# Changing the order of the tokens round a recurrence: in the matmuls' moving side instead of in copies and products

## The chip, the core and the metric

The kernel runs on one NeuronCore of a Trainium2 chip. A core has five engines that run side by side and meet at semaphores: TensorE (PE: matrix products out of SBUF into PSUM; its weight loads are listed as PEld), VectorE (DVE: elementwise work), ScalarE (ACT: functions of one argument), GpSimd (POOL) and SyncE (SP), of which the last two mostly issue DMAs here. SBUF and PSUM hold 128 partitions; an instruction names a pattern of elements along the partition, the same for all 128. The metric is the device time of one execution in microseconds (us).

A matmul has a stationary side, 128 x 128 weights that are loaded into the array, and a moving side, here up to 512 columns, which is read from SBUF and streamed past the weights. The result of each column is added up in a PSUM bank. The products here are in float32 precision: each operand is split into a high part (rounded to the type fp32r) and a low part, and every product is three matmuls: high x high, high x low, low x high.

## What is computed

One decoder layer on 512 tokens of width 1024: a SwiGLU layer, a mixer, another SwiGLU layer, each with norms around it. The mixer runs an attention branch and a recurrent branch on the same normed input `u` and merges them with gates. Only the recurrent branch matters here:

```python
xc  = causal_conv4(u @ w_in[:, xr], conv_w) + conv_b      # width 4, along the tokens
gate_x, gate_a = sigmoid(heads(xc) @ w_x + b_x), sigmoid(heads(xc) @ w_a + b_a)
log_a = -8 * gate_a * softplus(-a_param)
a, b  = exp(log_a), sqrt(-expm1(2 * log_a)) * gate_x * xc
h_t   = a_t * h_{t-1} + b_t                               # the recurrence, token by token
rec   = h * gelu(u @ w_in[:, yr])
rec_d = rec @ w_rec_branch
merged = gate0 * attn_d + gate1 * rec_d                   # gates from u @ w_in[:, gl]
```

The convolution and the recurrence run along the tokens, so they need the tokens in the order of time. The matrix products before and after do not care for the order.

## The kernel before

Activations are kept transposed: features on the 128 partitions, the 512 tokens along the free dimension. The tokens are not in the order of time there. Token number 4 i + p stands in column 128 p + i (p = 0 to 3, i = 0 to 127), an order that suits the dilated attention. Call it phase order; the other one is the order of time. Two views translate between them: `pi` reads a tile of 512 columns as (p, i) with 128 neighbours in the inner dimension, `ip` reads it as the same (p, i) where neighbouring i are four floats (16 bytes) apart.

The stage of the recurrent branch begins at about 638 us and ends at about 836 us of the span. Its order is written out (line 1493 on): `conv(0)`, and then for each of four heads `branch`, the load of the head's gate weights, `conv` of the next head, `gates_of`, `recur`, and some of the merge gates (line 1504). After the last head come the eight products with `w_rec_branch` (line 1512). Each head has two blocks of 128 features, so each of these routines works on two tiles of 128 x 512.

- `gemm` (lines 294 to 298) multiplies a block of 8 x 128 x 128 weights with the eight tiles of an activation: for each of eight tiles three matmuls of 512 columns (lines 279 to 281), 24 matmuls in all, into one PSUM bank.
- `conv` (line 1419): one `gemm` of `um`, the normed input in phase order; ScalarE copies the bank into `xr`, reading phase order and writing the order of time (line 1427, through `ip` and `pi`). The rest of the convolution is one ScalarE and three VectorE operations, then `split` makes high and low parts of the result in `rec` (lines 264, 265).
- `branch` (line 1435): one `gemm` of `um`; VectorE copies the bank into `ge`, which stays in phase order (line 1443).
- `gates_of` (line 1447): the head's small matmuls on `rec`, in the order of time, and sigmoids.
- `recur` (line 1463): elementwise work in the order of time, then the scan (line 1489) into `th`. Line 1490 multiplies `th`, read through `ip`, with `ge`, and writes `ge`: from here on everything is in phase order again. `split` writes it over `rec` (line 1491).
- Line 1504: the merge gates, `gemm` of `um`, sigmoid; phase order throughout.
- Lines 1512 to 1515: `gemm` of `rec`, the multiply with the merge gate in `sig` and the sum with the attention branch, all in phase order.

Weights come in by DMA in one stream, through two `raw` buffers (line 210); `fetch` splits them into high and low parts, with ScalarE and VectorE, some way ahead of their use. A planner places each engine's instructions from its own costs and from the priorities in the code; copies out of PSUM have a raised one (`EVAC`).

Of the kernel before, what the change touches and what calls it, by code (L numbers as in the profile page):

```python
# [12 lines left out]
AF = mybir.ActivationFunctionType  # L13
# [4 lines left out]
T = 512  # L18
# [131 lines left out]
def hybrid_layer(ctx: ExitStack, tc: tile.TileContext, xT: bass.AP, xN: bass.AP, wst: bass.AP,  # L150
                 first: bass.AP, rows: bass.AP, wdn: bass.AP, wbig: bass.AP, consts: bass.AP, bias: bass.AP, out: bass.AP):
    nc = tc.nc
    DVE, ACT, PE = nc.vector, nc.scalar, nc.tensor
# [68 lines left out]
    def fetch(key, slot=None, ahead=0):  # L222

        with tc.high_priority(offset=ahead if slot else AHEAD):
            src = raw_of(key)
            w = src.shape[-1]
            t = slot() if slot else w8() if w > 512 else w4()
            split(t[:, 0, :w], t[:, 1, :w], src)
            return t[:, 0, :w], t[:, 1, :w]

    def w8():
        return wpool.tile([P, 2, 1024], F32R, name="w8", tag="w8", bufs=4)
# [45 lines left out]
    def mm3(ps, wh, wl, xh, xl, first, last):  # L278
        PE.matmul(ps, wh, xh, start=first, stop=False)  # L279
        PE.matmul(ps, wh, xl, start=False, stop=False)  # L280
        PE.matmul(ps, wl, xh, start=False, stop=last)  # L281
# [9 lines left out]
        ts = [big([P, 2, 2, T]) for _ in range(4)]  # L291
        return Act([ts[k // 2][:, 0, k % 2, :] for k in range(8)], [ts[k // 2][:, 1, k % 2, :] for k in range(8)])

    def gemm(ps, wt, x, sl=slice(0, T), n=None):
        n = n or x.n
        a, b = k128(wt[0], n), k128(wt[1], n)
        for k in range(n):
            mm3(ps, a[:, k, :], b[:, k, :], x.hi[k][:, sl], x.lo[k][:, sl], k == 0, k == n - 1)

    def gemm_first(keys, x, slots, then):  # L300

# [443 lines left out]
    class Home:  # L745
# [15 lines left out]
        def slot(self, i):  # L761
            return self.act[:, 2 * i:2 * i + 2, :]
# [368 lines left out]
    um = act_of(um_t[:2], um_t[2:])  # L1131
# [15 lines left out]
    with ExitStack() as mx:  # L1147
# [228 lines left out]
        for c in range(KC):  # L1376
            ps = acc_ps()
# [3 lines left out]
    with ExitStack() as mx:  # L1381
        rpool = mx.enter_context(tc.tile_pool(name="rec", bufs=1))
        rec_t = rpool.tile([P, 16, T], F32R, name="rec")
        rec = Act([rec_t[:, i, :] for i in range(8)], [rec_t[:, 8 + i, :] for i in range(8)])
        sig = rpool.tile([P, KC, T], F32, name="sig")
        lpool_cm = tc.tile_pool(name="lru", bufs=1)
        lpool = lpool_cm.__enter__()


        def s8(name):  # L1390
            return lpool.tile([P, 8], F32, name=name)
        o, w = SMALL["ap"]
        av = sm[:, o:o + w]
        na, ab, ex, zz, z2, po = (s8(n) for n in ("na", "ab", "ex", "zz", "z2", "po"))
        sp4, sp8 = s8("sp4"), s8("sp8")
        DVE.tensor_scalar(na, av, -1.0, None, op0=ALU.mult)
        DVE.tensor_tensor(ab, av, na, op=ALU.min)
        ACT.activation(ex, ab, AF.Exp)
        DVE.tensor_scalar(zz, ex, 2.0, None, op0=ALU.add)
        DVE.reciprocal(zz, zz)  # L1400
        DVE.tensor_mul(zz, zz, ex)
        DVE.tensor_mul(z2, zz, zz)
        DVE.memset(po, 1.0 / 19.0)
        for i in (17, 15, 13, 11, 9, 7, 5, 3, 1):
            DVE.tensor_mul(po, po, z2)
            DVE.tensor_scalar(po, po, 1.0 / i, None, op0=ALU.add)
        DVE.tensor_mul(po, po, zz)
        DVE.tensor_scalar(na, na, 0.0, None, op0=ALU.max)
        DVE.scalar_tensor_tensor(po, po, 2.0, na, op0=ALU.mult, op1=ALU.add)
        DVE.tensor_scalar(sp4, po, 4.0, None, op0=ALU.mult)  # L1410
        DVE.tensor_scalar(sp8, po, -8.0, None, op0=ALU.mult)

        def ip(ap):
            return ap.rearrange("q (i p) -> q p i", p=4)

        def pi(ap):
            return ap.rearrange("q (p i) -> q p i", p=4)

        def conv(hd):

            for c in (2 * hd, 2 * hd + 1):
                ps = acc_ps()
                gemm(ps, fetch(("in", 36 + c)), um)
                xr = lpool.tile([P, 3 + T], F32, name="xr", tag="xr", bufs=2)
                DVE.memset(xr[:, 0:3], 0.0)
                with tc.high_priority(offset=EVAC):
                    ACT.activation(ip(xr[:, 3:]), pi(ps), AF.Copy)
                xc = sig[:, c, :]
                ACT.activation(xc, xr[:, 3:], AF.Identity, bias=col("cb", c), scale=col("cw", 3 * 8 + c))
                for t in (2, 1, 0):  # L1430
                    DVE.scalar_tensor_tensor(xc, xr[:, t:t + T], col("cw", t * 8 + c), xc,
                                             op0=ALU.mult, op1=ALU.add)
                split(rec.hi[c], rec.lo[c], xc)

        def branch(hd):

            gel = []
            for c in (2 * hd, 2 * hd + 1):
                ps = acc_ps()
                gemm(ps, fetch(("in", 44 + c)), um)  # L1440
                ge = lpool.tile([P, T], F32, name="ge", tag="ge", bufs=4)
                with tc.high_priority(offset=EVAC):
                    DVE.tensor_copy(ge, ps)
                gel.append(ge)
            return gel

        def gates_of(hd, wh, wl):
            a_ = wh.rearrange("p (w i c) -> p w i c", w=2, i=2)
            b_ = wl.rearrange("p (w i c) -> p w i c", w=2, i=2)
            gs = {}  # L1450
            for w, bn in ((1, "ba"), (0, "bx")):
                for j in range(2):
                    ps = aux_ps()
                    for i in range(2):
                        js = slice(j * P, (j + 1) * P)
                        mm3(ps, a_[:, w, i, js], b_[:, w, i, js], rec.hi[2 * hd + i], rec.lo[2 * hd + i],
                            i == 0, i == 1)
                    g = lpool.tile([P, T], F32, name="gt", tag="gt", bufs=6)
                    ACT.activation(g, ps, AF.Sigmoid, bias=col(bn, 2 * hd + j))
                    gs[w, j] = g  # L1460
            return [gs[1, j] for j in range(2)], [gs[0, j] for j in range(2)]

        def recur(hd, gel, gas, gxs):

            cs = (2 * hd, 2 * hd + 1)
            ths, rs = [tmp("th") for _ in cs], [tmp("r0") for _ in cs]
            for c, th, ga in zip(cs, ths, gas):
                ACT.activation(th, ga, AF.Tanh, scale=sp4[:, c:c + 1])  # L1470
            for c, r0, ga in zip(cs, rs, gas):
                ACT.activation(r0, ga, AF.Exp, scale=sp8[:, c:c + 1])
            for r0, th, ga in zip(rs, ths, gas):
                ACT.activation(r0, r0, AF.Copy, bias=0.5, scale=0.5)
                DVE.scalar_tensor_tensor(ga, th, 1.0, r0, op0=ALU.add, op1=ALU.mult)
                DVE.scalar_tensor_tensor(r0, ga, 2.0, r0, op0=ALU.subtract, op1=ALU.mult)
                DVE.tensor_mul(ga, th, r0)
            for c, gx in zip(cs, gxs):
                DVE.tensor_mul(gx, gx, sig[:, c, :])
            for th in ths:  # L1480
                ACT.activation(th, th, AF.Sqrt)
            for ga in gas:
                ACT.activation(ga, ga, AF.Copy, bias=1.0, scale=2.0)
            for ge in gel:
                ACT.activation(ge, ge, AF.Gelu_apprx_tanh)
            for c, r0, th, ga, gx, ge in zip(cs, rs, ths, gas, gxs, gel):
                DVE.scalar_tensor_tensor(th, th, -2.0, r0, op0=ALU.mult, op1=ALU.mult)
                DVE.tensor_mul(gx, gx, th)
                DVE.tensor_tensor_scan(th, ga, gx, 0.0, op0=ALU.mult, op1=ALU.add)
                DVE.tensor_mul(pi(ge), ip(th), pi(ge))  # L1490
                split(rec.hi[c], rec.lo[c], ge)

        turns.update(n=4, of=(4, 5, 6, 7), aux=0)
        conv(0)
        for hd in range(NH):
            gel = branch(hd)
            lru = fetch(("lru", hd))
            if hd + 1 < NH:
                conv(hd + 1)
            gas, gxs = gates_of(hd, *lru)  # L1500
            recur(hd, gel, gas, gxs)
            for c in GATE1[hd]:
                ps = acc_ps()
                gemm(ps, fetch(("in", 60 + c)), um)
                ACT.activation(sig[:, c, :], ps, AF.Sigmoid)
        lpool_cm.__exit__(None, None, None)
        turns.update(n=5, of=(5, 6, 7))

        mg = act_big("mg")
        for c in range(KC):  # L1510
            ps = acc_ps()
            gemm(ps, fetch(("rec", c)), rec)
            DVE.tensor_mul(sig[:, c, :], ps, sig[:, c, :])
            DVE.tensor_add(sig[:, c, :], sig[:, c, :], facc[:, c, :])
            split(mg.hi[c], mg.lo[c], sig[:, c, :])
# [149 lines left out]
```

## Time and profile before

| | |
|---|---|
| median of 2 runs | 1230.96 us (1230.32 to 1231.6) |
| the profiled execution | 1229.78 us, of it the span 1228.0 us |
| granted TensorE clock, mean over the span | 0.998 |
| busy: TensorE, weight loads, VectorE, ScalarE | 1213.7, 1094.4, 961.2, 740.6 us |
| stage of the recurrent branch | 637.7 to about 836 us |

The profile is that of one execution, whose span runs from the first to the last instruction. A row of a group of instructions gives the line, the engine and operation, output <- inputs, shape and count, then the busy time in us and the mean duration of one in ns, then the time that the engine stood idle just before such instructions and who ended it. A row of a wait reads: engine, tile and line <- who released it: total us, times, longest us. The timeline lists start and duration in us. Matmuls overlap each other, so that the duration of one (390 ns) is longer than the step from one to the next.

### The profile page before, as it was taken

How to read it: one execution, taken by the hardware profiler on the slowest of the kernel's cores; microseconds unless marked ns; L12 is line 12 of the kernel's file. 1: busy time of each engine (PE TensorE's matmuls, PEld its weight loads, DVE VectorE, ACT ScalarE, POOL GpSimd, SP SyncE). 2: the span in 40 equal slices, each digit the busy share in tenths (PEclk: the TensorE clock that was granted, in tenths of full speed). 3: DMA queues.
4: the chain of work that ended last, by engine and by line, in shares of the span. 5: the costliest groups of instructions: out<-in, count | busy, mean ns of one | idle time of the engine just before them, and what ended most of it. 6: DMA issues, size and time to landing. Idle time of an engine off the chain costs nothing.

```text
span 1228.0 us, 18986 instructions
## 1 busy us (share of the span) xinstructions
PE 1213.7 (99%) x7556; PEld 1094.4 (89%) x7556; DVE 961.2 (78%) x1504; ACT 740.6 (60%) x1229; POOL 75.6 (6%) x123
## 2 busy tenths in 40 slices
PE   9999999999999999999999999999999999999997
PEld 8898989999878999999988878888899999999996
DVE  7998778988579888888566878655788887979864
ACT  6566665655556564666545878734566665656452
POOL 0001111100102000000000000000110010101000
PEclk9999999999999999999999999999999999999999
DMA  6336646464725322222252222324463555455441
GB/s 245 137 104 172 170 110 175 142 164 119 258 103 166 115 91 91 78 78 104 85 190 73 99 103 69 133 77 166 147 197 104 152 155 153 151 146 159 117 155 69
DMA packets 36025, 163.40 MB, mean 133 GB/s; under 512 B 3936, under 2 KB 7136, under 8 KB 23904
## 3 DMA queue, kind: packets, MB, share of 16 engines
q1 hardware_dynamic: 18288, 107.13, 24.9%
q0 software_dynamic: 17648, 55.06, 17.4%
q8 instruction: 59, 0.97, 0.3%
q14 instruction: 30, 0.25, 0.1%
HBM read 151.69 MB, written 6.29 MB: 129 GB/s over the span
## 4 chain that ended last, share of the span: by engine, by line
PE 84%; DVE 8%; ACT 4%; issue 2%; DMA 2%; SPq 0%; DVEq 0%; ACTq 0%
PE bank L972 9%; PE bank L973 9%; PE bank L974 9%; PE bank L281 5%; PE bank L279 5%; PE bank L280 5%; PE bank L639 4%; PE bank L640 4%; PE bank L641 4%; PE bank L887 4%; PE bank L886 4%; PE bank L888 4%; PE bank L393 3%; PE bank L392 3%; PE bank L394 3%
## 5 line engine op out<-in xcount | busy, mean ns | idle before, releaser
L265 DVE TENSOR_TENSOR w<-raw,w 128x1024 fp32r<-128x1024 f32 (+1 forms) x273 | 295.4, 1093 | 68.7 <-ACT w L264 65.0
L264 ACT ACTIVATE w<-raw 128x1024 fp32r<-128x1024 f32 (+1 forms) x273 | 254.1, 951 | 105.3 <-PE bank L281 50.4
L972 PE MATMUL bank<-big,w 128*128 128x256 f32 x816 | 233.8, 286 | 3.0 <-DVE u L985 1.3
L973 PE MATMUL bank<-big,w 128*128 128x256 f32 x816 | 230.7, 283 | 0.0
L974 PE MATMUL bank<-big,w 128*128 128x256 f32 x816 | 229.4, 283 | 0.0
L972 PEld LDWEIGHTS bank<-big,w 128*128 128x128 f32 x816 | 156.1, 191 | 7.9 <-DVE u L985 2.0
L973 PEld LDWEIGHTS bank<-big,w 128*128 128x128 f32 x816 | 156.2, 191 | 1.6
L974 PEld LDWEIGHTS bank<-big,w 128*128 128x128 f32 x816 | 155.6, 191 | 0.0
L639 PE MATMUL bank<-big,w 128*128 128x256 f32 x320 | 91.8, 287 | 0.0
L640 PE MATMUL bank<-big,w 128*128 128x256 f32 x320 | 91.7, 287 | 0.0
L641 PE MATMUL bank<-big,w 128*128 128x256 f32 x320 | 90.8, 284 | 0.0
L886 PE MATMUL bank<-wd,act 128*128 128x512 f32 x224 | 87.8, 392 | 0.0
L887 PE MATMUL bank<-wd,act 128*128 128x512 f32 x224 | 87.7, 392 | 0.0
L888 PE MATMUL bank<-wd,act 128*128 128x512 f32 x224 | 87.2, 389 | 0.0
L281 PE MATMUL bank<-big,w 128*128 128x512 f32 x192 | 74.8, 390 | 2.1 <-DVE w L265 2.1
L280 PE MATMUL bank<-big,w 128*128 128x512 f32 x192 | 74.7, 389 | 0.0
L279 PE MATMUL bank<-big,w 128*128 128x512 f32 x192 | 74.7, 390 | 0.0
L281 PE MATMUL bank<-act,w 128*128 128x512 f32 (+1 forms) x184 | 64.7, 352 | 0.0
L280 PE MATMUL bank<-act,w 128*128 128x512 f32 (+1 forms) x184 | 64.7, 352 | 0.0
L279 PE MATMUL bank<-act,w 128*128 128x512 f32 (+1 forms) x184 | 64.7, 355 | 0.0
L980 ACT ACTIVATE c<-bank 128x256 f32<-128x256 f32 x70 | 26.6, 381 | 61.2 <-PE bank L974 60.8
L639 PEld LDWEIGHTS bank<-big,w 128*128 128x128 f32 x320 | 61.2, 191 | 1.0
(375 smaller groups left out, 2964.2 us busy)
## 6 DMA issues: line engine op xcount, KB each, us to landing
raw<-in_w SPq DMA_DIRECT2D x90, 1024.0 KB, 4.9
dr<-in_wdn POOLq DMA_DIRECT2D x40, 512.0 KB, 5.4
npair<-in_wdn POOLq DMA_DIRECT2D x32, 512.0 KB, 5.4
big<-act POOLq DMA_DIRECT2D x6, 512.0 KB, 3.2
h<-in_x SPq DMA_DIRECT2D x8, 256.0 KB, 5.2
h<-in_xn POOLq DMA_DIRECT2D x4, 512.0 KB, 5.8
raw<-in_wbig SPq DMA_DIRECT2D x2, 1024.0 KB, 4.7
kept_m<-h POOLq DMA_DIRECT2D x4, 512.0 KB, 2.9
```

The source lines that it names most:

```text
L264: ACT.activation(dh, src, AF.Copy)
L265: DVE.tensor_sub(dl, src, dh.bitcast(F32))
L279: PE.matmul(ps, wh, xh, start=first, stop=False)
L280: PE.matmul(ps, wh, xl, start=False, stop=False)
L281: PE.matmul(ps, wl, xh, start=False, stop=last)
L639: PE.matmul(ps, wh, xh, start=start and k == 0, stop=False, skip_group_check=True)
L640: PE.matmul(ps, wh, xl, start=False, stop=False, skip_group_check=True)
L641: PE.matmul(ps, wl, xh, start=False, stop=k == 3, skip_group_check=True)
L886: PE.matmul(ps, xh, wh, start=start and k == 0, stop=False, skip_group_check=True)
L972: PE.matmul(ps, wh, xh, start=start and k == 0, stop=False, skip_group_check=True)
L973: PE.matmul(ps, wh, xl, start=False, stop=False, skip_group_check=True)
L974: i = PE.matmul(ps, wl, xh, start=False, stop=k == 3, skip_group_check=True)
```

## The change

`gemm` gets a view `seen` that is laid over the moving sides of its matmuls. A new view `timed` reads a phase-ordered tile in the order of time: the inner dimension has the four p, 128 floats (512 bytes) apart, and after four of them the next i follows.

- The products of `conv` and of `branch` read `um` through `timed`, so that their banks hold the order of time. The ScalarE copy into `xr` (line 1427) becomes a copy of 512 neighbours, and `ge` is in the order of time too.
- The product of line 1490 then has all three tiles in the order of time, 512 neighbours each, and `rec` stays in the order of time.
- The products of line 1512 read `rec` through `ip` (16 bytes from one element to the next), so that their banks are in phase order as before.

Nothing is added to or taken from the list of instructions; their patterns of elements change. The merge gates (line 1504) and the matmuls of `gates_of` keep theirs.

```diff
-    def gemm(ps, wt, x, sl=slice(0, T), n=None):
+    def gemm(ps, wt, x, sl=slice(0, T), n=None, seen=lambda ap: ap):
         n = n or x.n
         a, b = k128(wt[0], n), k128(wt[1], n)
         for k in range(n):
-            mm3(ps, a[:, k, :], b[:, k, :], x.hi[k][:, sl], x.lo[k][:, sl], k == 0, k == n - 1)
+            mm3(ps, a[:, k, :], b[:, k, :], seen(x.hi[k][:, sl]), seen(x.lo[k][:, sl]), k == 0, k == n - 1)
...
+        def timed(ap):
+            return ap.rearrange("q (p i) -> q i p", p=4)
+
         def conv(hd):
 
             for c in (2 * hd, 2 * hd + 1):
                 ps = acc_ps()
-                gemm(ps, fetch(("in", 36 + c)), um)
+                gemm(ps, fetch(("in", 36 + c)), um, seen=timed)
...
-                    ACT.activation(ip(xr[:, 3:]), pi(ps), AF.Copy)
+                    ACT.activation(xr[:, 3:], ps, AF.Copy)
...
-                gemm(ps, fetch(("in", 44 + c)), um)
+                gemm(ps, fetch(("in", 44 + c)), um, seen=timed)
...
                 DVE.tensor_tensor_scan(th, ga, gx, 0.0, op0=ALU.mult, op1=ALU.add)
-                DVE.tensor_mul(pi(ge), ip(th), pi(ge))
+                DVE.tensor_mul(ge, th, ge)
                 split(rec.hi[c], rec.lo[c], ge)
...
-            gemm(ps, fetch(("rec", c)), rec)
+            gemm(ps, fetch(("rec", c)), rec, seen=ip)
```

## The prediction

> **What bounds the kernel now.** I read the page's head, the busy times and the chain that ended last.
>
> ```profile
> span 1228.0 us, 18986 instructions
> PE 1213.7 (99%) x7556; PEld 1094.4 (89%) x7556; DVE 961.2 (78%) x1504; ACT 740.6 (60%) x1229; POOL 75.6 (6%) x123
> PE 84%; DVE 8%; ACT 4%; issue 2%; DMA 2%; SPq 0%; DVEq 0%; ACTq 0%
> ```
>
> TensorE is busy 99% of the span, and only 14 us of it are gaps. Whatever is taken from other engines can return at most such a gap. So I ask two things of the changed stage: how many TensorE gaps lie in it, and what its matmuls cost. The busy times of the stage, of a stretch inside it, and the waits of the stage:
>
> ```profile
> 637.00:836.00 199.00, 196.89 (x869) 162.47 (x868) 138.20 (x178) 135.27 (x172) 0.00 (x0) 1.00 0.28 99
> 740.00:760.00 20.00, 20.00 (x90) 16.57 (x89) 15.67 (x21) 19.87 (x27) 0.00 (x0) 1.00 0.31 106
> ACT w L264 <- PE bank L281: 31.9, 10, 3.9
> DVE sig L1513 <- PE bank L281: 19.0, 8, 3.0
> ACT xr L1427 <- PE bank L281: 13.1, 4, 4.9
> PE bank L281 <- DVE w L265: 2.1, 1, 2.1
> ```
>
> The columns of the first two rows are stretch, length, then busy time of PE, weight loads, VectorE, ScalarE, GpSimd, then the granted clock (1.00). TensorE waits once in 199 us, for 2.1 us. ScalarE and VectorE wait for TensorE far longer (31.9, 19.0 and 13.1 us). The stage goes at the rate of its matmuls. That rate is read from their starts:
>
> ```profile
> 701.67 0.39 PE L279 MATMUL bank<-rec,w 128*128 128x512 f32 x1
> ...
> 714.81 0.39 PE L280 MATMUL bank<-big,w 128*128 128x512 f32 x1
> ```
>
> Between these two starts the timeline lists 58 steps from one matmul to the next: 13.14 us / 58 = 226.6 ns each. (The 0.39 us of one matmul overlaps the next one; only the step counts.)
>
> **The change part by part.**
>
> *The matmuls that change.* The weight columns of lines 1423, 1440 and 1512 are each 8 matrix products of 8 x 3 matmuls: 3 x 8 x 24 = 576 matmuls. The gate products (192) and the recurrence's own gate matmuls (96) keep contiguous moving sides. Together that is 864, and 864 x 226.6 ns + 2.1 us = 197.9 us, which is the stage. The rows of the same groups:
>
> ```profile
> L281 PE MATMUL bank<-big,w 128*128 128x512 f32 x192 | 74.8, 390 | 2.1 <-DVE w L265 2.1
> L279 PE MATMUL bank<-rec,w 128*128 128x512 f32 x96 | 37.3, 389 | 0.0
> ```
>
> Three such rows each (lines 279 to 281) make 576 on `big`, of which 384 change, and 288 on `rec`, of which 192 change. The 576 changed ones take 576 x 0.2266 = 130.5 us now. No matmul is added or removed; what changes is that each of 512 elements read per partition lies 512 bytes (lines 1423, 1440; after four such it goes back to the next float) or 16 bytes (line 1512) from the one before, where now they are neighbours. No matmul of the trace reads its moving side like that, so its price has to be bounded from other engines.
>
> *Rows nearest to it.* The very operations that the change makes contiguous walk SBUF in steps of 16 bytes, four floats. First ScalarE (PSUM to SBUF copies; line 1427 writes with that step, the others contiguously), then VectorE (SBUF to SBUF; line 1490 reads with that step):
>
> ```profile
> L980 ACT ACTIVATE c<-bank 128x256 f32<-128x256 f32 x70 | 26.6, 381 | 61.2 <-PE bank L974 60.8
> L1175 ACT ACTIVATE vals<-bank 128x512 f32<-128x512 f32 x4 | 2.4, 598 | 0.0
> L1427 ACT ACTIVATE xr<-bank 128x512 f32<-128x512 f32 x8 | 8.7, 1086 | 13.1 <-PE bank L281 13.1
> L265 DVE TENSOR_TENSOR w<-raw,w 128x512 fp32r<-128x512 f32 x65 | 44.5, 686 | 4.4 <-ACT w L264 4.3
> L265 DVE TENSOR_TENSOR w<-raw,w 128x1024 fp32r<-128x1024 f32 x208 | 252.9, 1220 | 64.3 <-ACT w L264 60.7 <-PE bank L641 3.2
> L1490 DVE TENSOR_TENSOR ge<-th,ge 128x512 f32<-128x512 f32 x8 | 8.5, 1067 | 0.0
> ```
>
> ScalarE: 256 elements more cost 598 - 381 = 217 ns, 0.85 ns each, so the fixed part is 598 - 512 x 0.85 = 164 ns, and the stepped copy took (1086 - 164) / 512 = 1.80 ns per element. VectorE: (1220 - 686) / 512 = 1.04 ns, fixed 686 - 534 = 152 ns, and the stepped product (1067 - 152) / 512 = 1.79 ns per element. **Two engines of different speed (0.85 and 1.04 ns) come down to the same 1.8 ns.** Were the penalty "two of the engine's own cycles", they would stand at 1.70 and 2.08. I take from it that the memory sets the price: some 1.8 ns for each element that lies in another small piece of SBUF.
>
> *Price of a changed matmul.* Lowest: nothing, if TensorE's reads are fed otherwise; its time then stays at 226.6 ns. By the ratio of each engine to itself: 1.79/1.04 = 1.72 to 1.80/0.85 = 2.12, so 390 to 480 ns. By the difference that the step adds to 512 elements: 1067 - 686 = 381 to 1086 - 598 = 488 ns, so 608 to 715 ns. By the memory's own price: 512 x 1.79 = 916 ns. Highest: a whole stepped instruction, 1086 ns; but that holds a fixed part which matmuls in a row overlap, so I leave it out. I choose 916 ns, since the agreement of the two engines in nanoseconds is the one feature of the rows that the other readings leave unexplained, and a matmul asks at 0.44 ns per element for more than either engine does.
>
> [...]
>
> *What is taken away.* Eight ScalarE copies fall from 1086 to about 598 ns (3.9 us), eight VectorE products from 1067 to about 686 ns (3.0 us). Both lie beside TensorE's work, except in the one place where TensorE waited. The chain of work ahead of it:
>
> ```profile
> 670.57 0.99 ACT xr L1427
> ...
> 721.37 0.99 DVE ge L1490
> ...
> 724.66 0.98 DVE ge L1490
> 725.64 1.14 DVE w L265
> 726.83 0.50 PE bank L281
> ```
>
> One copy and two products of the kinds that get shorter stand in this chain: 0.49 + 2 x 0.38 = 1.25 us of the 2.1 us wait. With matmuls four times as long in this stretch, ScalarE and VectorE (135 and 138 us busy in a stage of some 590 us) are never late and the whole 2.1 us goes. Nothing else is late next: TensorE itself is.
>
> *The rest.* No DMA, no wait and no buffer is added, and nothing is moved past a queue; the copy of line 1443 and the multiply of line 1513 keep their shapes. The planner may reorder a few operations on ScalarE and VectorE, at nothing, since both idle for TensorE by the waits above. Weight loads of 0.19 us lie under longer matmuls.
>
> *The sum.* The profiled execution took 1229.8 us, its span 1228.0; 1.8 us lie around it. 576 x (0.916 - 0.2266) = +397.1, less 2.1: 1229.8 + 395.0 = **1624.8 us**, rounded 1625. The two runs shown have the median 1231.0, 1.2 us above that execution; I don't add it.
>
> **The rivals.**
>
> *Each engine pays in its own cycles.* TensorE then needs 1.72 to 2.12 times its 226.6 ns: 163 to 254 ns more, x 576 = +94 to +146 us: 1322 to 1374 us, about 1358 at exactly double. For it: both ratios stand near two. Against it: the 1.8 ns that both share.
>
> *The step adds a fixed delay per element.* +381 to +488 ns a matmul, x 576 = +219 to +281: 1447 to 1509 us. It would also be about the time if only one of the two steps (512 bytes on 384 matmuls) costs: 384 x 0.689 = +265. Against it: the delays of the two engines differ by a quarter while their totals per element agree.
>
> *The moving side is fed whatever its step is: not slower.* [...] Then the stage keeps its 130.5 us, and 1.25 to 2.1 us of the wait go: 1229.8 - 1.7 = 1228 us. More than 2.1 us isn't to be had in this stage. For it: the trace shows no stepped matmul to refute it. Against it: it must deliver four times what two engines get (1.8 / 0.44). [...]
>
> [...]
>
> **How the numbers follow.** Memory's price 0.42 (1610 to 1645 us); own cycles 0.29 (1322 to 1374); fixed delay or one step alone 0.09 (1447 to 1509); free 0.16 (1228); worse 0.04. The likeliest gives 1625 us. The range leaves out the free case and the worst one, 0.20 together: 1320 to 1650 us; it is that wide since the price of a stepped moving side lies between ends far apart. About 2% is what a measurement of this kernel can tell from no change, 24.6 us. The free case lies within it (0.15, with 0.01 for a gain beyond what I can find); all others are slower by more than 7%: 0.84.
>
> **What would show it.** In the changed profile the starts of matmuls in lines 1423, 1440 and 1512 stand 0.9 us apart (0.45 by the second reading, 0.23 if free), while those of line 1504 still stand at 0.227. Lines 1427 and 1490 show about 600 and 686 ns. The wait of line 281 for VectorE is gone, ScalarE and VectorE wait longer for TensorE, and the busy times outside the stage are unchanged. I am wrong if TensorE's reader isn't bound like those of the other two, or if it is bound in its own cycles; both would be seen in the step between matmuls alone.

## The result: 5% slower, and where the time is

The changed kernel takes 1293.99 us (two runs, 1293.96 and 1294.01) against 1230.96 us: a ratio of 1.0514, 95% interval 1.0498 to 1.0531. It is slower, as forecast, but by 63 us and not by 394; 1294 us lies under the stated range.

The head of the page after, and its chain that ended last:

```profile
span 1292.2 us, 18986 instructions
PE 1280.1 (99%) x7556; PEld 1100.1 (85%) x7556; DVE 958.3 (74%) x1504; ACT 738.2 (57%) x1229; POOL 75.6 (6%) x123
PE 89%; DVE 5%; ACT 2%; DMA 2%; issue 2%; DVEq 0%; SPq 0%; ACTq 0%
```

The span grew by 64.2 us and TensorE's busy time by 66.4, with the same 7556 matmuls. VectorE and ScalarE lost 2.9 and 2.4 us of busy time. To see where it lies, the busy times in three stretches, before first (the middle row, of 637 to 836 us, stands in the prediction), then after (columns as there):

```profile
0.00:637.00 637.00, 631.87 (x4165) 578.74 (x4166) 521.36 (x862) 381.55 (x680) 41.92 (x72) 1.00 0.44 137
...
836.00:1228.00 392.00, 384.91 (x2526) 353.18 (x2524) 301.61 (x465) 223.81 (x379) 33.67 (x51) 0.99 0.48 144
```
```profile
0.00:637.00 637.00, 631.87 (x4164) 578.49 (x4165) 521.16 (x862) 381.55 (x680) 41.95 (x72) 1.00 0.43 137
637.00:900.00 263.00, 263.00 (x869) 168.18 (x868) 135.49 (x178) 132.55 (x172) 0.00 (x0) 1.00 0.21 75
900.00:1292.00 392.00, 385.19 (x2527) 353.40 (x2525) 301.69 (x465) 224.07 (x379) 33.70 (x51) 1.00 0.47 144
```

Both ends of the kernel are unchanged; the stage of the recurrence went from 199 to 263 us with the same count of matmuls and a full clock. TensorE waits for nothing in it now. Inside the stage the timeline shows three steps between matmuls: the products with the stepped `um`, the unchanged gate products, and the products with the stepped `rec`:

```profile
640.27 0.45 PE L280 MATMUL bank<-big,w 128*128 128x512 f32 x1
...
671.72 0.45 PE L281 MATMUL bank<-big,w 128*128 128x512 f32 x1
...
759.97 0.39 PE L281 MATMUL bank<-big,w 128*128 128x512 f32 x1
...
770.17 0.39 PE L281 MATMUL bank<-big,w 128*128 128x512 f32 x1
...
839.68 0.64 PE L281 MATMUL bank<-rec,w 128*128 128x512 f32 x1
...
859.92 0.64 PE L280 MATMUL bank<-rec,w 128*128 128x512 f32 x1
```

From 640.27 to 671.72 there are 111 steps: **283.3 ns**. From 759.97 to 770.17 there are 45: 226.7 ns, as before. From 839.68 to 859.92 there are 44: **460.0 ns**. So the steps of 512 bytes cost 1.25 times and those of 16 bytes 2.03 times the contiguous price. The sum over the 576 matmuls is 384 x 56.7 + 192 x 233.4 = 21.8 + 44.8 = 66.6 us; less the 2.1 us wait that went, 64.5 us. Measured: 64.2.

The waits after (of the stretch from 630 to 900 us) confirm who sets the pace:

```profile
ACT w L264 <- PE bank L281: 80.2, 16, 9.0
DVE sig L1516 <- PE bank L281: 63.9, 8, 8.7
ACT xr L1430 <- PE bank L281: 26.7, 8, 6.5
```

They were 31.9, 19.0 and 13.1 us. (One wait of the first row lies ahead of 637 us; without it the row has 78.2 us.) The copy and the product that were to become cheaper did (median of eight each, listed by line as min/median/max ns): 598 ns, from 1084, and 682 ns, from 1065.

```profile
L1430 ACT ACTIVATE xr<-bank x8: 597/598/602, 645.3 to 754.3; 128x512 f32<-128x512 f32 x8
L1493 DVE TENSOR_TENSOR ge<-th,ge x8: 664/682/693, 702.4 to 807.4; 128x512 f32<-128x512 f32 x8
```

### The profile page after: what moved, and what is told of

It reads as the page before. It is cut to its first block, busy times and chain, and to the rows that moved or that the text cites. A ratio compares the mean times of both kernels' runs of the same rounds, so it can differ in the third digit from the quotient of the medians.

```text
span 1292.2 us, 18986 instructions
## 1 busy us (share of the span) xinstructions
PE 1280.1 (99%) x7556; PEld 1100.1 (85%) x7556; DVE 958.3 (74%) x1504; ACT 738.2 (57%) x1229; POOL 75.6 (6%) x123
## 4 chain that ended last, share of the span: by engine, by line
PE 89%; DVE 5%; ACT 2%; DMA 2%; issue 2%; DVEq 0%; SPq 0%; ACTq 0%
PE bank L972 9%; PE bank L279 8%; PE bank L280 8%; PE bank L281 8%; PE bank L973 8%; PE bank L974 8%; PE bank L639 4%; PE bank L640 4%; PE bank L641 4%; PE bank L887 4%; PE bank L886 4%; PE bank L888 4%; PE bank L394 3%; PE bank L393 3%; PE bank L392 3%
## 5 line engine op out<-in xcount | busy, mean ns | idle before, releaser
L281 PE MATMUL bank<-big,w 128*128 128x512 f32 x192 | 82.6, 430 | 0.0
L280 PE MATMUL bank<-big,w 128*128 128x512 f32 x192 | 82.6, 430 | 0.0
L279 PE MATMUL bank<-big,w 128*128 128x512 f32 x192 | 82.4, 430 | 0.0
```

## The experiments

The theory of the forecast, one new small piece of SBUF per 1.79 ns and element, fell: it asks 916 ns of both patterns. Two questions were left: do the two patterns simply add up, and what sets their two prices?

### One pattern at a time

With `um` alone read in the order of time, VectorE brings the recurrence's result back to phase order:

```diff
-                DVE.tensor_mul(ge, th, ge)
-                split(rec.hi[c], rec.lo[c], ge)
+                DVE.tensor_mul(pi(gx), ip(th), ip(ge))
+                split(rec.hi[c], rec.lo[c], gx)
...
-            gemm(ps, fetch(("rec", c)), rec, seen=ip)
+            gemm(ps, fetch(("rec", c)), rec)
```

> Only the 384 matmuls of conv and branch read um in the order of time (steps of 512 bytes, four to a run); VectorE's product goes back to phase order (both inputs stepped, contiguous output), and the rec products read contiguously. Theory A (each matmul pays by its own pattern, and nothing else matters): these matmuls start 283 ns apart, the rec products 227 ns apart; 384 x 57 ns = 22 us over the kernel before, less up to 2 us of the wait: 1250 us. Theory B (the 512-byte pattern is dear only beside the other edits, or the whole loss is in the rec products): within 3 us of the kernel before.

With `rec` alone stepped, the two copies out of PSUM write the order of time:

```diff
-                gemm(ps, fetch(("in", 36 + c)), um, seen=timed)
+                gemm(ps, fetch(("in", 36 + c)), um)
...
-                    ACT.activation(xr[:, 3:], ps, AF.Copy)
+                    ACT.activation(ip(xr[:, 3:]), pi(ps), AF.Copy)
...
-                gemm(ps, fetch(("in", 44 + c)), um, seen=timed)
+                gemm(ps, fetch(("in", 44 + c)), um)
...
-                    DVE.tensor_copy(ge, ps)
+                    DVE.tensor_copy(ip(ge), pi(ps))
```

> Only the 192 matmuls of the rec products read with steps of 16 bytes; conv and branch read um contiguously, and ScalarE and VectorE write the order of time with steps of 16 bytes as they evict. Theory A (each matmul pays by its own pattern): the rec products start 460 ns apart and conv and branch 227 ns apart; 192 x 233 ns = 45 us over the kernel before: 1274 us, so that this and the run with um alone add up to the whole change. Theory B (both patterns share one cost): anything clearly under 40 us.

Measured against the kernel before (1231.13 us beside them): 1248.80 us, ratio 1.0143 (1.0122 to 1.0163), and 1274.12 us, ratio 1.0342 (1.0321 to 1.0362). The spans are 1247.1 and 1273.0 us, 19.1 and 45.0 over 1228.0; together 64.1, and the whole change has 64.2. The steps between matmuls say the same. Two neighbouring matmuls with the stepped `um` from the first run, then two with the stepped `rec` from the second:

```profile
645.06 0.45 PE L281 MATMUL bank<-big,w 128*128 128x512 f32 x1
645.34 0.45 PE L279 MATMUL bank<-big,w 128*128 128x512 f32 x1
```
```profile
830.10 0.64 PE L281 MATMUL bank<-rec,w 128*128 128x512 f32 x1
830.56 0.64 PE L279 MATMUL bank<-rec,w 128*128 128x512 f32 x1
```

They start 0.28 and 0.46 us apart, while the products of `rec` in the first run and those of `um` in the second stay at 0.22 to 0.23. Theory A holds: each matmul pays by its own pattern, and the two patterns account for the whole change to within 0.1 us. The wait of 2.1 us is gone in the first and still 1.5 us in the second, where ScalarE and VectorE write in steps.

### What a step costs

Rows of 16 equal matmuls behind the last product of `rec`, one row for each pattern, on `rec` as it lies there (`flat` is its 8192 elements per partition, of 4 bytes each). Five more rows take a copy in bf16, a type of 2 bytes:

```diff
+        for r in range(16): PE.matmul(bp, bw, flat[:, :512], start=r == 0, stop=r == 15)
...
+        for r in range(16): PE.matmul(bp, bw, flat[:, :2048].rearrange('q (i s) -> q i s', s=4)[:, :, 0], start=r == 0, stop=r == 15)
...
+        for r in range(16): PE.matmul(bp, bw, flat[:, :512].rearrange('q (p i) -> q i p', p=8), start=r == 0, stop=r == 15)
...
+        for r in range(4): q = tmp('bq'); ACT.activation(tip(q), tim(bp), AF.Copy)
```

Here L and R are two theories of the price, and their numbers are steps from start to start in ns.

> The kernel before, with rows of 16 equal matmuls of 512 fp32r columns put in behind the rec products, one row for each pattern of the moving side (their sums are used by nothing), then ScalarE copies and VectorE products of 512 elements with the same patterns, and five rows of bf16 matmuls. [...] L, a price of 0.9 ns for each new piece of 16 bytes, with the last few pieces held: contiguous 227; steps of 8 bytes 227, 12 bytes 345, 16, 32 and 64 bytes 460; the order of time (inner 4, 512 bytes) 283 and inner 2 less, inner 8, 16 and 32 rising to 460; 64 elements in steps of 512 bytes 460; inner 4 without coming back to the same pieces 460; runs of two or four neighbours 227. [...] R, a price of 0.44 ns for each start of an inner run: inner 2 340, inner 4 283, inner 8 255, inner 32 234, inner 4 without coming back 283, runs of four neighbours 283, runs of two 340. For ScalarE and VectorE, L expects the order of time to cost much less than steps of 16 bytes (1086 and 1067 ns), R no more than a quarter over contiguous.

Listed by line: count, min/median/max ns, first and last start in us. The step is the difference of the starts over 15 (over 14 in the first bf16 row, whose first matmul is missing from the trace); starts are listed to 0.1 us, so that a step is good to some 7 ns. Here contiguous, steps of 8 and of 16 bytes; then the patterns with 2, 4 and 8 tracks (a track is a run of neighbours; 4 tracks is the order of time); then bf16 contiguous and with steps of 4, 8 and 16 bytes:

```profile
L1522 PE MATMUL bank<-rec x16: 389/389/389, 837.0 to 840.4; 128*128 128x512 f32 x16
L1524 PE MATMUL bank<-rec x16: 615/630/637, 840.6 to 847.4; 128*128 128x512 f32 x16
L1528 PE MATMUL bank<-rec x16: 644/645/645, 855.1 to 862.0; 128*128 128x512 f32 x16
L1536 PE MATMUL bank<-rec x16: 379/379/403, 883.6 to 886.9; 128*128 128x512 f32 x16
L1538 PE MATMUL bank<-rec x16: 434/451/451, 887.1 to 891.3; 128*128 128x512 f32 x16
L1540 PE MATMUL bank<-rec x16: 667/667/724, 891.6 to 899.0; 128*128 128x512 f32 x16
L1556 PE MATMUL bank<-facc x15: 379/379/379, 941.2 to 944.3; 128*128 128x512 bf16 x15
L1558 PE MATMUL bank<-facc x16: 386/387/388, 944.5 to 947.9; 128*128 128x512 bf16 x16
L1560 PE MATMUL bank<-facc x16: 611/629/632, 948.1 to 954.9; 128*128 128x512 bf16 x16
L1562 PE MATMUL bank<-facc x15: 1078/1078/1078, 955.3 to 968.8; 128*128 128x512 bf16 x15
```

In order: 227, 453 and 460 ns; 220, 280 and 493; bf16 about 220, then 227, 453 and 900. The other fp32r rows: steps of 12 bytes 447, of 32 and 64 bytes 433; 16 and 32 tracks 433; runs of four neighbours 240, runs of two (8 bytes out of every 16) 447; 64 elements in steps of 512 bytes 553; four tracks whose elements lie 16 bytes apart, so that no piece comes back, 487.

Both theories miss. L put steps of 8 bytes at 227: 453. R put runs of two at 340 and eight tracks at 255: 447 and 493. Steps of 8 to 64 bytes cost about the same, 433 to 460; only the steps of 512 bytes stand out, at 553, and why is open. What stands out is bf16: the price doubles with each doubling of the step from 4 to 16 bytes, to 900 / 512 = 1.76 ns per element when each lies in another 16 bytes, and then stays (920 ns with steps of 32 bytes, at a granted clock of 0.50). That is close to the 1.79 ns which the forecast took from VectorE and ScalarE. fp32r pays half of that, 460 ns, and pays it already at 8 bytes (453).

ScalarE and VectorE behave otherwise, and here too the two theories miss. Out of SBUF, in steps of 16 bytes and then in the order of time, one row of each:

```profile
L1569 ACT ACTIVATE bq<-rec x4: 1112/1130/1147, 796.5 to 801.0; 128x512 f32<-128x512 f32 x4
L1581 DVE TENSOR_TENSOR bq<-rec,sig x4: 1022/1028/1078, 1009.7 to 1012.6; 128x512 f32<-128x512 f32 x4
```

The other two medians are 1147 ns (ScalarE, order of time) and 1054 (VectorE, steps of 16 bytes). L expected the order of time to be much cheaper than steps of 16 bytes, R at most a quarter over contiguous (617 and 693 ns): it costs these two engines the full price, though the pattern is back in the same 16 bytes four elements later. Steps of 8 bytes, for which TensorE paid 453 against 227, cost them 660 and 684 ns, next to nothing.

### A count of even and odd columns

No trace lists how a matmul's moving side is read; the runs show a price for each pattern. An estimate of mine, made from the rows above, puts most of them into one count: of the elements, count those that lie in another piece of 16 bytes than the one before (16, since the bf16 price stops rising there), and take 1.77 ns for each (453 / 256; in bf16 900 / 512 = 1.76). In bf16 the count goes over all columns; in fp32r over the even columns alone (the odd ones give the same number). Where it gives less than 220 ns, as for two tracks, the rows took 220. Steps of 8 bytes in fp32r: the even columns are 16 bytes apart, 256 new pieces, 453 ns. Contiguous, they have two elements in each piece: 128 pieces, 227 ns. A flat price of 0.88 ns (453 / 512) for each element of a stepped moving side would give the steps of 8 bytes as well. Two tracks with steps of 8 bytes tell the two apart, since each half of the columns then stays on one track, with two elements to a piece: 227 by the count, 453 by the flat price.

```diff
+        for r in range(16): PE.matmul(bp, flat[:, :P], flat[:, :1024].rearrange('q (i s) -> q i s', s=2)[:, :, 0], start=r == 0, stop=r == 15)
...
+        for r in range(16): PE.matmul(bp, flat[:, :P], flat[:, :1024].rearrange('q (p i s) -> q i p s', p=2, s=2)[:, :, :, 0], start=r == 0, stop=r == 15)
```

> The kernel before with rows of 16 equal matmuls behind the rec products, as in the run with the patterns; a track is a row of neighbouring elements, and a pattern of two tracks takes one element from each in turn. [...]

The rows, in order: one track of 8-byte steps, two tracks of 8-byte steps, two tracks of 16-byte steps, two tracks of pairs, four tracks; then bf16 with two and four tracks:

```profile
L1523 PE MATMUL bank<-rec x16: 615/630/637, 840.7 to 847.5; 128*128 128x512 f32 x16
L1525 PE MATMUL bank<-rec x16: 389/389/414, 848.0 to 851.4; 128*128 128x512 f32 x16
L1527 PE MATMUL bank<-rec x16: 615/630/637, 851.6 to 858.4; 128*128 128x512 f32 x16
L1529 PE MATMUL bank<-rec x16: 502/507/514, 858.9 to 863.9; 128*128 128x512 f32 x16
L1531 PE MATMUL bank<-rec x16: 447/451/451, 864.2 to 868.4; 128*128 128x512 f32 x16
L1541 PE MATMUL bank<-facc x16: 644/646/647, 885.8 to 893.1; 128*128 128x512 bf16 x16
L1543 PE MATMUL bank<-facc x16: 1027/1042/1043, 893.6 to 906.5; 128*128 128x512 bf16 x16
```

453, **227**, 453, 333, 280, and bf16 487 and 860 ns. The count is right where it differs most from the flat price: 227 against 453. Four tracks that lie 512, 528 and 2048 bytes apart cost 280, 273 and 280. The count fits; why the halves would count by themselves is not shown.

It leaves some numbers open. Pairs stand at 333: it gives 453 if every change from one track to the other is counted, and 227 if a return to the same piece is free. And tracks in bf16 fit neither: 906 ns if every change is counted, the contiguous 220 if a return is free. Four tracks (860) lie near the first, two (487) in the middle, and two tracks in steps of 4 bytes cost 540. (Runs of four bf16 neighbours touch 128 pieces, which is 227. The row gave 287, but it stands behind the row of 860, and the granted clock was 0.61 from 903.5 to 911 us; its median duration, 388 ns, is that of the bf16 row of 227 ns, 387.)

### Why does the order of time cost 280 ns?

With four tracks, each half of the columns goes to and fro between two. The count is 227 ns if a return to the same piece is free, and 453 if it is paid in full. It costs 280. Does it matter whether the two tracks come to new pieces within the same four columns? The distance between the tracks decides whether they do:

```diff
+        for r in range(16): PE.matmul(bp, flat[:, :P], flat[:, :512].rearrange('q (p i) -> q i p', p=4)[:, :128, :], start=r == 0, stop=r == 15)
...
+        for r in range(16): PE.matmul(bp, flat[:, :P], flat[:, :516].rearrange('q (p i) -> q i p', p=4)[:, :128, :], start=r == 0, stop=r == 15)
```

> The kernel before with rows of 16 equal fp32r matmuls behind the rec products, to tell why four tracks cost 280 ns and not 227 or 453. [...]

Four tracks at 128, 129, 130 and 131 floats from each other, then eight at 64 and 65:

```profile
L1522 PE MATMUL bank<-rec x16: 435/451/451, 842.9 to 847.2; 128*128 128x512 f32 x16
L1524 PE MATMUL bank<-rec x16: 392/397/403, 847.4 to 851.0; 128*128 128x512 f32 x16
L1526 PE MATMUL bank<-rec x16: 438/442/447, 851.2 to 855.3; 128*128 128x512 f32 x16
L1528 PE MATMUL bank<-rec x16: 397/397/398, 855.6 to 859.1; 128*128 128x512 f32 x16
L1532 PE MATMUL bank<-rec x16: 667/667/721, 863.7 to 871.0; 128*128 128x512 f32 x16
L1534 PE MATMUL bank<-rec x16: 617/617/627, 871.5 to 878.1; 128*128 128x512 f32 x16
```

287, 240, 273 and 233 ns, then 487 and 440. When the two tracks of one half of the columns come to new pieces in different fours of columns (129 and 131), the order of time costs next to nothing, 233 to 240, where a contiguous row that starts 8 bytes later costs 233 too. When they come together (128, 130, and 136 at 273), it costs a fifth to a quarter more. Six tracks, three to a half, cost 293 (510 columns, in the run before). Eight tracks, four to a half, cost 487 at a distance of 64 floats and 433 to 440 at 65, 66 and 72.

That is not the whole account. Two tracks of pairs cost 333 as they are, and 333 when the second is shifted by two floats, so that the two tracks of a half come to new pieces in turn. Four tracks of 8-byte steps cost 333, and 327 with a shift that left the two tracks of each half in step (516 floats apart). Shown is that the distance between tracks sets the price of the order of time; how it does so is not shown.

### A version that beats both

The rows of the run with the patterns also list ScalarE and VectorE (ScalarE out of SBUF, then out of PSUM, in the order of time; VectorE out of PSUM in steps of 16 bytes):

```profile
L1570 ACT ACTIVATE bq<-rec x4: 1135/1147/1154, 802.0 to 805.0; 128x512 f32<-128x512 f32 x4
L1575 ACT ACTIVATE bq<-bank x4: 680/696/716, 993.1 to 994.6; 128x512 f32<-128x512 f32 x4
L1585 DVE TENSOR_TENSOR bq<-bank,sig x4: 679/679/680, 1023.0 to 1024.8; 128x512 f32<-128x512 f32 x4
```

Steps are dear where these two read SBUF (1130 to 1147 ns for ScalarE, 1028 to 1054 for VectorE) or write it (1146 to 1192 and 1040 to 1077 out of SBUF), against 617 and 693 contiguous, and cheap where they read PSUM (contiguous: 601 and 677 ns out of PSUM, so a sixth more for ScalarE and nothing for VectorE). Every bank is read once by one of them anyway, so all changes of order can be made there:

```diff
-                    ACT.activation(ip(xr[:, 3:]), pi(ps), AF.Copy)
+                    ACT.activation(tip(xr[:, 3:]), timed(ps), AF.Copy)
...
-                    DVE.tensor_copy(ge, ps)
+                    DVE.tensor_copy(tip(ge), timed(ps))
...
-                DVE.tensor_mul(pi(ge), ip(th), pi(ge))
+                DVE.tensor_mul(ge, th, ge)
...
-            DVE.tensor_mul(sig[:, c, :], ps, sig[:, c, :])
+            DVE.tensor_mul(pi(sig[:, c, :]), ip(ps), pi(sig[:, c, :]))
```

> The matmuls read contiguously as in the kernel before, and every change of order is made where ScalarE or VectorE reads PSUM: the copy into xr reads its bank in the order of time and writes neighbours, the copy into ge reads its bank in the order of time, the recurrence's last product is contiguous, and the multiply of the rec products' banks with the merge gate reads them in phase order. By the rows of the run with the patterns (ScalarE out of PSUM in the order of time 696 ns against 1086 for writing SBUF in steps; VectorE out of PSUM in steps 679 ns against 677), eight copies fall by 0.39 us and eight products by 0.38 us, at no matmul. Theory A (the one wait of TensorE, 2.1 us, ends with that chain of ScalarE and VectorE): it shrinks by 1 to 2.1 us, to 1229 to 1230 us, 0.1 to 0.2% under the kernel before. Theory B (the wait hangs on something else): no difference.

Measured: 1228.18 us (1227.68 to 1229.44) against 1230.70 beside it, ratio 0.9976, interval 0.9965 to 0.9986. It is faster than both kernels, if only by 0.24% than the one before: its eight runs all lie under the twelve beside them (1229.83 us at the least). Its copy into `xr` takes as long as a contiguous one, the multiply with the merge gate 692 ns as before, and in the stage no wait of TensorE on line 281 is left:

```profile
span 1226.7 us, 18986 instructions
L1433 ACT ACTIVATE xr<-bank x8: 581/598/599, 644.6 to 736.4; 128x512 f32<-128x512 f32 x8
PE bank L455 <- DVE u L447: 0.2, 1, 0.2
```

Theory A's wait is the one that went. The span is 1.3 us shorter than the 1228.0 of the profile before; the medians differ by 2.5 us, which is more than theory A's 2.1, but the interval (1.7 to 4.3 us) reaches down to it.

## Why the prediction was wrong

- *What bounds the kernel*: right. TensorE sets the stage's time; the copies and products that got 0.49 and 0.38 us shorter gave back no more than the 2.1 us wait, as the sum had it, and the other engines waited longer. That the change is slower was no luck: stepped reads of SBUF do cost TensorE time (283 and 460 ns a matmul against 227). Only how much was wrong.
- *Which matmuls change, and how many*: right. 576 of them, and the unchanged 288 still start 226.7 ns apart; the two prices found here add up to 64.5 us, and the span grew by 64.2.
- *The price of a changed matmul*: this is the step that failed, "by the memory's own price: 512 x 1.79 = 916 ns". It was the one term that mattered, and it was mis-sized for both patterns: 283 and 460 ns. Two assumptions of it were wrong. First, that TensorE pays per element what VectorE pays. In bf16 it does (900 ns), but in fp32r it pays half of that (460 ns): what ScalarE and VectorE share in nanoseconds came back in bf16 and did not carry over to fp32r. Second, that every element of the order of time costs a new piece. It lies in another piece than the one before, but four columns later the pattern is back, and TensorE doesn't pay in full again: 280 ns, where the count takes 453 if every change is paid. The forecast said itself that the pattern "goes back to the next float" after four steps, and then priced it like the other one. No row of the kernel before could have told: ScalarE and VectorE pay the full price in this order too (1147 and 1028 ns). What it did allow was a price, and a range, for each pattern by itself.
- *The bounds*: "nothing" to 1086 ns held both prices. The readings in between gave one price to both patterns, and so the range, built from cases of that kind, began at 1320 and missed 1294. The case "own cycles" has the 16-byte price (2.03 against 1.72 to 2.12), but for the wrong reason, since the step of 8 bytes costs as much (453 ns) and bf16 twice as much (900 ns); its time of 1322 to 1374 was missed because it too charged the 384 matmuls in the order of time in full. The case of one pattern alone picked the wrong one, the 512-byte steps, which turned out the cheaper.
- *The case "not slower"*: refuted by both patterns of the change (283 and 460 ns). It isn't wrong of every pattern: two tracks 1024 bytes apart cost 220 ns, no more than contiguous.
- *The case "worse"* (0.04, above 1650 us): no run shows its price. The 512-byte steps of the change were the cheaper pattern, and the dearest fp32r row, 64 elements in steps of 512 bytes, cost 553 ns.
- *What would show it*: the step between matmuls alone decided it, as said.

## What to carry to other kernels

Count, for a moving side that isn't contiguous, how many elements lie in another piece of 16 bytes than the one before, in fp32r for the even columns alone, and whether the pattern comes back to a piece soon: that count, an estimate from the rows here, orders those of 220, 280 and 460 ns better than the size of the step does, though it doesn't give the pairs (333) or the tracks in bf16 (487 and 860). Where TensorE is the bound, an order is better changed where ScalarE or VectorE reads PSUM, which cost 696 against 601 ns and 679 against 677 in the rows, and nothing in the kernel that does it (598 and 692 ns, as contiguous). A price that two engines share (1.8 ns per element here) may still not be that of a third (0.90 ns, 460 / 512, in fp32r); where one unknown price carries the whole sum, its range should be set by the count of each pattern by itself.

## What the runs showed of the hardware beside this

- The order of time with tracks 129 floats apart costs 240 ns against 280 to 287 at 128: in these rows a pad of one float to a track takes most of the price away. No kernel here uses it.
- The granted clock fell in bf16 rows of few, long matmuls, though TensorE counted as busy. The stretches with steps of 8 bytes, then of 16 bytes, then the contiguous fp32r row behind them:

```profile
948.50:954.50 6.00, 6.00 (x15) 1.60 (x14) 0.00 (x0) 0.00 (x0) 0.00 (x0) 1.00 0.00 0
955.50:958.00 2.50, 1.78 (x2) 0.23 (x2) 0.00 (x0) 0.00 (x0) 0.00 (x0) 1.00 0.00 0
962.00:968.50 6.50, 6.50 (x8) 0.89 (x7) 0.00 (x0) 0.00 (x0) 0.00 (x0) 0.50 0.00 0
984.00:989.00 5.00, 5.00 (x17) 3.70 (x16) 0.00 (x0) 0.00 (x0) 0.00 (x0) 0.74 0.00 0
```

The clock is the third number from the end: 1.00, 1.00, 0.50, 0.74. (One matmul record is missing in the second stretch.) The matmuls of 16-byte steps took 0.89 us each already at the full clock (two in 1.78 us), so that the fall is not what made them slow; but the contiguous row behind them started 360 ns apart on average instead of 227. The clock fell also round the bf16 row of 860 ns (0.61 from 903.5 to 911 us), and not in the rows of 453 to 553 ns (1.00). What the clock goes by is not shown.
